# Routing's rest as a side chain, one ring of weight buffers instead of two, and the identity first, in a two-layer decoder trunk

## Chip, core and metric

One core of one Trainium2 chip runs the whole program. The metric is device time in microseconds (us). A profiled execution also gives a trace, whose span runs from its first to its last instruction. TensorE is called PE here, VectorE DVE, ScalarE ACT, GpSimd POOL; SP is the engine that issues the weight loads.

## The reference

256 tokens of width 1024 go through two layers. Layer 0 is multi-head latent attention and a dense SwiGLU, layer 1 is gated DeltaNet and a mixture of 8 experts, of which each token takes 2. The change lies in the experts and, with one edit, at the very start.

```python
def moe_ffn(h, w_router, w_gate_up, w_down):
    t = h.reshape(B * S, D)                        # 256 x 1024
    top_val, top_idx = lax.top_k(t @ w_router, 2)  # of 8
    top_w = jax.nn.softmax(top_val, axis=-1)
    combine = jnp.sum(one_hot(top_idx, 8) * top_w[..., None], axis=1)
    for e in range(8):
        gt, up = jnp.split(t @ w_gate_up[e], 2, axis=-1)      # 1024 x 2816, float32
        out = out + combine[:, e:e+1] * ((silu(gt) * up) @ w_down[e])   # 1408 x 1024
```

The eight experts' weights are 138.4 MB of float32, 17.3 MB for each expert.

## The kernel before

**Experts by size.** A sort by token count gives the eight experts seats 0 to 7. Even seats are big ("B", up to 128 tokens), odd ones small ("S", up to 64 tokens); expert 0 always has seat 0. A second pass for experts with more tokens stands in a branch that these inputs don't take. The kernel gathers each expert's tokens by a matmul with a one-hot matrix `P` (`place`, L1821, writes its columns on DVE; `gather`, L1850, does the matmuls in 9 steps), computes gate, up and down, and adds the result back by a matmul with the transpose of `P`. `places_back` (L1830) makes that transpose `SM` and the weight of every gathered token, `wsl`, which needs the routing weights `cmb2`.

**Weights.** An expert's weights come in 35 tiles of 128 x 1024 or 128 x 768 float32: 24 of gate and up, 11 of down. A big expert splits each tile in a high part (ACT cast, L197) and a low part (DVE subtraction, L198) and multiplies three times (L2046 gate and up; L1962 to L1964 down). A small expert feeds the raw tiles to PE (L2076, L1979).

**Two rings.** `wload` (L180) takes a raw buffer and issues the load on SP. Gate and up tiles take one of the 10 buffers of `wrw`; down tiles, in `down_raw` (L1931), one of the 6 of `wr2`. A load waits until the last reader of its buffer is done, and SP works in order.

**Routing.** After the router's matmul the kernel ranks the experts of each token, and positions come by a matmul (L1718 to L1724). `place(0)` and `gather(0)` make the tokens of seat 0. Then `between()`, that is `routed()` (L1755), does the rest in one piece: the second maximum and its exponential, the count per expert (`cnt`), the sort (`perm`), the arrays by seat (`chosS`, `posS`, `eidS`, `cntS`), the experts' numbers for SP (`eidi`), the routing weights (`cmb2`) and the overflow test (`mosti`). After it all the other experts' places are written, 14 instructions on DVE.

**Order.** Inside `manual_schedule` (L116 to `order.close()`, L2098) PE, DVE, ACT and POOL keep the written order among the instructions of the block. After that, and for SP throughout, the framework's planner orders the instructions by written order and by its own forecast of when each is ready; the order is then fixed.

**Side work.** While an expert's gate and up run, `sides(more)` (L2030) is called nine times (ten in a small expert), after chosen tiles, and advances every side chain by one step: the scatter of the expert before, the gather of the next group of seats (groups (0), (1,2), (3,4), (5,6,7); a group starts one expert before its first seat) and, for seat 0, `places_back()` of all eight seats.

**PSUM.** In the experts' stage 5 banks go by the tag "mm" and 3 by "acc"; the two results of a big expert's down (`y0`, `y1`) and the banks `psw` and `st` of `places_back` take "acc".

**Start.** POOL issues nine small loads (L102 to L113) and then writes the identity (L118, L119) that PE's first transpose (L141) reads.

Of the kernel before, what the change touches and what calls it, by code (L numbers as in the profile page):

```python
# [16 lines left out]
D = 1024  # L17
# [12 lines left out]
NE = 8  # L30
# [19 lines left out]
def hybrid_kernel(ctx: ExitStack, tc: tile.TileContext, rope_rows, x, c, positions, ada_w, ada_b,  # L50
# [40 lines left out]
    nc.sync.dma_start(xtok, x.rearrange("o (t p) d -> p (o t) d", p=128))  # L91

    rows = sm.tile([39, 128], F32, name="rows", bufs=1)
    r0 = 0
    col_of = {}
    for name, ap in (("nm", norm_mix.rearrange("l (k p) -> (l k) p", p=128)),
# [19 lines left out]
    order.enter_context(tc.manual_schedule(engines=MANUAL))  # L116
    ident = cst.tile([128, 128], F32)
    nc.gpsimd.memset(ident, 0.0)  # L118
    nc.gpsimd.affine_select(out=ident, in_=ident, pattern=[[-1, 128]], base=0, channel_multiplier=1,  # L119
                            compare_op=OP.not_equal, fill=1.0)  # L120
    upper = cst.tile([128, 128], F32)
# [1624 lines left out]
    tge, perm = (sm.tile([128, NE, NE], F32, name=n, bufs=1) for n in ("tge", "perm"))  # L1746
    chosS, posS = rt("chosS"), rt("posS")
    eidi = cst.tile([1, NE], I32, name="eidi")
# [6 lines left out]
    def routed():  # L1755
# [15 lines left out]
        nc.vector.tensor_copy(cnt, pt[:, 0:NE])  # L1771
        nc.vector.tensor_copy(cntm, cnt)
        nc.vector.memset(cntm[:, 0:1], -1.0)
        sq3 = [128, NE, NE]
        mine, other = cntm[:, :, None].to_broadcast(sq3), cntm[:, None, :].to_broadcast(sq3)
# [5 lines left out]
        nc.vector.tensor_tensor(perm, want[:, :, None].to_broadcast(sq3), trank[:, None, :].to_broadcast(sq3),  # L1781
                                op=OP.is_equal)
        by_turn(chosS, chos)
        by_turn(posS, pos)
        for o, v in ((eidS, eids), (cntS, cnt)):
            nc.vector.tensor_tensor(tge, perm, v[:, None, :].to_broadcast(sq3), op=OP.mult)
            nc.vector.reduce_sum(o, tge, axis=AX.X)
        nc.vector.tensor_copy(eidi, eidS[0:1, :])
        w1 = sm.tile([128, 2, 1], F32, name="w1", bufs=1)
        nc.vector.tensor_scalar(w1, w2, 1.0, None, op0=OP.add)  # L1790
        nc.vector.reciprocal(w1, w1)
        nc.vector.tensor_tensor(w2, w2, w1, op=OP.mult)
        comb = sm.tile([128, 2, NE], F32, name="comb", bufs=1)
        nc.vector.tensor_tensor(comb, chos, oh0, op=OP.subtract)
        nc.vector.tensor_tensor(comb, comb, w2.to_broadcast([128, 2, NE]), op=OP.mult)
# [4 lines left out]
        nc.vector.tensor_tensor(cmb2[:, :, :, 1], oh0, cmb2[:, :, :, 0].bitcast(F32), op=OP.subtract)  # L1800

        nc.vector.tensor_tensor(cntS, cntS, caps, op=OP.subtract)
        most = sm.tile([128, 1], F32, name="most", bufs=1)
        nc.vector.reduce_max(most, cntS, axis=AX.X)
        nc.vector.tensor_scalar(most, most, 128.0, None, op0=OP.add)
        nc.vector.tensor_copy(mosti, most[0:1, :])

    def experts(again, between):
# [20 lines left out]

        def places_back():  # L1830
            psw = acc_bank("psw")
            for e in range(NE):
                pt = acc_bank("st")
                parts = [places[e]] if kinds[e] == "B" else [places[e], places[e] + 128]
                for h, o in enumerate(parts):
                    for t in range(2):
                        pl = P[:, t, o:o + 128]
                        mm(pt[:, h * S + t * 128:h * S + (t + 1) * 128], lhsT=pl, rhs=identr, start=True, stop=True)
                        mm(psw[:, 2 * e:2 * e + 2], lhsT=pl, rhs=cmb2[:, t, e, :], start=h == t == 0,
                           stop=h == len(parts) - 1 and t == 1)  # L1840
# [4 lines left out]
            nc.vector.tensor_copy(pw, psw[:, :2 * NE].rearrange("p (e c) -> p e c", c=2))  # L1845
            nc.vector.tensor_tensor(wsl, pw[:, :, 0], pw[:, :, 1], op=OP.add)

# [83 lines left out]
        def down_raw(e, f):  # L1931
            w = moe_w_down[0, 0] if e == 0 else moe_w_down[0, bass.ds(expert_of(e), 1)].rearrange("e r c -> (e r) c")
            if kinds[e] == "S" and f == 9:

                return wload(lambda t: [(t[0:64], w[9 * 128 + 64:10 * 128, :]), (t[64:128], w[9 * 128:9 * 128 + 64, :])],
                             [128, D], ring=wr2)
            return wload(lambda t: [(t, w[f * 128:(f + 1) * 128, :])], [128, D], ring=wr2)

# [7 lines left out]

        def y_halves(e):
            if e == NE - 1:
                nc.scalar.activation(warmed, wsl[:, 0:1], AF.Sqrt, bias=eps_t, scale=0.0)
            return [sm.tile([128, D], F32R, name=n, tag=n, bufs=1) for n in ("yh", "yl")]  # L1950

        def down(e, f0, n, ah, al):
# [12 lines left out]
            if f0 + n // 128 < nf:  # L1965
                return
            yh, yl = y_halves(e)
            for q in range(2):
# [3 lines left out]
        def down_small(e, blocks):  # L1972
# [8 lines left out]
            if blocks[-1][0] == nf - 1:  # L1981
                yh, yl = y_halves(e)
                weigh(e, slice(0, 512), (yh, yl, yps[e]))
                outs.append(scatter(e, yh, yl))
# [73 lines left out]
        def expert_small(e, more):  # L2058
# [3 lines left out]
            for c0 in (0, 1024):  # L2062
# [23 lines left out]
                after()  # L2086

        if again:
            for e in range(NE):
                place(e, ps_of, chosS)  # L2090
            list(gather(0))
# [100 lines left out]
```

## Time and profile before

| what | value |
|---|---|
| runs | 1030.16, 1029.38, 1021.74 us; median 1029.38 |
| profiled execution | 1026.9 us; its span 1025.1 us |
| busy share of the span | PE 92%, DVE 66%, ACT 48%, POOL 12% |
| moved | 261.33 MB, mean 255 GB/s |
| mean granted clock of PE | 0.959 of full |

The span is 1.8 us shorter than the execution. Time 0 is the span's first instruction. The experts run from about 595 us to about 1007 us, a final norm follows. A timeline row gives start, duration, engine, line, operation, output<-input and count, and in brackets the engine's idle time before it with what released it. Matmuls of one engine overlap, so their durations don't add up.

### The profile page before, as it was taken

How to read it: one execution, taken by the hardware profiler on the slowest of the kernel's cores; microseconds unless marked ns; L12 is line 12 of the kernel's file. 1: busy time of each engine (PE TensorE's matmuls, PEld its weight loads, DVE VectorE, ACT ScalarE, POOL GpSimd, SP SyncE). 2: the span in 40 equal slices, each digit the busy share in tenths (PEclk: the TensorE clock that was granted, in tenths of full speed). 3: DMA queues.
4: the chain of work that ended last, by engine and by line, in shares of the span. 5: the costliest groups of instructions: out<-in, count | busy, mean ns of one | idle time of the engine just before them, and what ended most of it. 6: DMA issues, size and time to landing. Idle time of an engine off the chain costs nothing. (4 is left out here: it accounts for less than half of the span.)

```text
span 1025.1 us, 18883 instructions
## 1 busy us (share of the span) xinstructions
PE 941.9 (92%) x6802; PEld 752.2 (73%) x6802; DVE 673.1 (66%) x1274; ACT 490.7 (48%) x879; POOL 123.9 (12%) x226
## 2 busy tenths in 40 slices
PE   5899999999999997999999779899999899989984
PEld 3787889999999997888899768745664576457431
DVE  5788948878786778877753566625864495358232
ACT  2367546443444466555544555723742473256212
POOL 2000001000000132535633400000000000000000
PEclk9999998999999989999999877999999999999997
DMA  9959994979988846422224463789999998999992
GB/s 303 366 169 327 289 314 141 319 247 332 331 279 284 266 138 191 124 83 84 84 84 144 145 209 106 239 302 325 366 372 364 347 363 329 355 352 361 366 328 69
DMA packets 152740, 261.33 MB, mean 255 GB/s; under 512 B 13650, under 2 KB 104832, under 8 KB 152640
## 3 DMA queue, kind: packets, MB, share of 16 engines
q1 hardware_dynamic: 152336, 259.81, 74.2%
q8 instruction: 55, 0.90, 0.4%
q0 software_dynamic: 304, 0.25, 0.2%
q14 instruction: 45, 0.37, 0.1%
HBM read 258.97 MB, written 1.05 MB: 254 GB/s over the span
## 5 line engine op out<-in xcount | busy, mean ns | idle before, releaser
L461 ACT CAST whi<-w 128x1024 fp32r<-128x1024 f32 (+3 forms) x147 | 138.5, 958 | 112.7 <-PE gu L1143 45.0
L198 DVE TENSOR_TENSOR wlo<-w,whi 128x1024 fp32r<-128x1024 f32 (+1 forms) x136 | 154.5, 1158 | 43.1 <-ACT whi L197 41.4
L466 DVE TENSOR_TENSOR wlo<-w,whi 128x1024 fp32r<-128x1024 f32 (+3 forms) x132 | 148.2, 1137 | 21.1 <-ACT whi L461 20.9
L197 ACT CAST whi<-w 128x1024 fp32r<-128x1024 f32 (+1 forms) x136 | 132.2, 998 | 42.3 <-DMA w<-in_moe_w_gate_up_dram 22.8
L1142 PE MATMUL gu<-hhi,whi 128*128 128x256 f32 x336 | 95.4, 284 | 0.0
L1144 PE MATMUL gu<-hhi,wlo 128*128 128x256 f32 x336 | 95.1, 283 | 0.0
L1143 PE MATMUL gu<-hlo,whi 128*128 128x256 f32 x336 | 95.1, 283 | 0.0
L2076 PE MATMUL gu<-w,XF 128*64 128x512 f32 (+1 forms) x384 | 84.4, 564 | 0.0
L230 PE MATMUL pj<-hhi,whi 128*128 128x256 f32 x240 | 73.5, 306 | 0.0
L232 PE MATMUL pj<-hhi,wlo 128*128 128x256 f32 x240 | 68.5, 286 | 3.8 <-DVE wlo L466 3.8
L2046 PE MATMUL gu<-whi,XH 128*128 128x512 f32 x192 | 61.2, 400 | 9.4 <-ACT whi L197 9.4
L231 PE MATMUL pj<-hlo,whi 128*128 128x256 f32 x240 | 68.4, 285 | 0.0
L466 POOL TENSOR_TENSOR wlo<-w,whi 128x1024 fp32r<-128x1024 f32 x15 | 39.4, 2626 | 225.9 <-DVE al L1117 181.0
L1143 PEld LDWEIGHTS gu<-hlo,whi 128*128 128x128 f32 x336 | 64.5, 192 | 0.0
L1142 PEld LDWEIGHTS gu<-hhi,whi 128*128 128x128 f32 x336 | 64.5, 192 | 0.0
L1144 PEld LDWEIGHTS gu<-hhi,wlo 128*128 128x128 f32 x336 | 64.5, 192 | 0.0
L2046 PE MATMUL gu<-wlo,XH 128*128 128x512 f32 x192 | 60.8, 398 | 1.0 <-DVE wlo L198 0.9
L2076 PEld LDWEIGHTS gu<-w,XF 128*64 128x64 f32 x384 | 26.4, 136 | 44.7 <-issue 40.2
L2046 PE MATMUL gu<-whi,XL 128*128 128x512 f32 x192 | 58.8, 387 | 0.0
L260 DVE SCALAR_TENSOR_TENSOR adacc<-adaw,csil,adacc 128x1024 f32<-128x1024 f32 x42 | 56.2, 1337 | 2.7 <-DMA adaw<-in_ada_w_dram 2.6
L1979 PE MATMUL y<-w,at 128*64 128x512 f32 x176 | 47.2, 635 | 6.7 <-DMA w<-in_moe_w_down_dram 6.6
L1922 POOL TENSOR_TENSOR xT<-xT,part 128x256 f32<-128x256 f32 x1 | 0.7, 725 | 414.5 <-PE fx L2125 414.5
(527 smaller groups left out, 2281.6 us busy)
## 6 DMA issues: line engine op xcount, KB each, us to landing
w<-in_moe_w_down_dram SPq DMA_DIRECT2D x84, 512.0 KB, 7.4
w<-in_moe_w_gate_up_dram SPq DMA_DIRECT2D x128, 256.0 KB, 5.4
w<-in_moe_w_gate_up_dram SPq DMA_DIRECT2D x64, 512.0 KB, 7.3
adaw<-in_ada_w_dram SPq DMA_DIRECT2D x50, 512.0 KB, 5.1
w<-in_moe_w_gate_up_dram SPq DMA_DIRECT2D x128, 192.0 KB, 4.1
w<-in_ada_w_dram SPq DMA_DIRECT2D x46, 512.0 KB, 6.8
w<-in_ffn_w_gate_up_dram SPq DMA_DIRECT2D x88, 256.0 KB, 5.3
w<-in_gdn_w_in_dram SPq DMA_DIRECT2D x32, 512.0 KB, 4.6
```

Of the source, the lines that this page charges most:

```text
L197: nc.scalar.copy(dv(hi), rv(raw))
L198: eng.tensor_tensor(dv(lo), rv(raw), dv(hi).bitcast(F32), op=OP.subtract)
L230: mm(ps, lhsT=lhi, rhs=rhi, start=first, stop=False)
L231: mm(ps, lhsT=lhi, rhs=rlo, start=False, stop=False)
L232: mm(ps, lhsT=llo, rhs=rhi, start=False, stop=last)
L461: nc.scalar.copy(dv(hi), rv(raw))
L466: eng.tensor_tensor(dv(lo), rv(raw), dv(hi).bitcast(F32), op=OP.subtract)
L1142: mm(o, lhsT=h[:, c], rhs=rh, start=k == g == 0 and new, stop=False, skip_group_check=True)
L1143: mm(o, lhsT=h[:, c], rhs=rl, start=False, stop=False, skip_group_check=True)
L1144: mm(o, lhsT=l[:, c], rhs=rh, start=False, stop=k == 1 and g == 3, skip_group_check=True)
L2046: mm(p[:, :2 * m].rearrange("p (g c) -> p g c", g=2), lhsT=x[:, kk, :], rhs=w[:, k, :, o:o + m], start=kk == i == 0, stop=kk == 7 and i == 2)
L2076: mm(o, lhsT=X[:, k, :], rhs=r, start=k == 0, stop=k == 7, tile_position=(0, 64 * h))
```

## The change

```diff
     nc.sync.dma_start(xtok, ...)
+    ident = cst.tile([128, 128], F32)
+    nc.gpsimd.memset(ident, 0.0)
+    nc.gpsimd.affine_select(out=ident, ...)
     rows = sm.tile([39, 128], F32, name="rows", bufs=1)
...
     order.enter_context(tc.manual_schedule(engines=MANUAL))
-    ident = cst.tile([128, 128], F32)
-    nc.gpsimd.memset(ident, 0.0)
-    nc.gpsimd.affine_select(out=ident, ...)
...
-    def wload(srcs, shape, name="w", ring=None):
-        raw = (ring or wrw).tile(shape, F32, name=name, tag="w")
+    def wload(srcs, shape, name="w"):
+        raw = (ring[0]() if ring else wrw).tile(shape, F32, name=name, tag="w")
...
+    nload = [0]
+    def in_turn():
+        nload[0] += 1
+        return wr2 if nload[0] % 8 in (0, 3, 6) else wrw
+    ring.append(in_turn)
...
     def routed():
...
         nc.vector.tensor_copy(cnt, pt[:, 0:NE])
+        nc.vector.tensor_copy(w2s, w2)
+
+    def turns_of():
...
+        yield
         by_turn(chosS, chos)
         by_turn(posS, pos)
-        for o, v in ((eidS, eids), (cntS, cnt)):
-            ...
+        ...              # eidS alone
         nc.vector.tensor_copy(eidi, eidS[0:1, :])
+        yield
+
+    def weights_of():    # w1 to comb, as before, on w2s
...
+        yield
         by_turn(oh0, comb)
...
         nc.vector.tensor_copy(mosti, most[0:1, :])
+        yield
...
-        def places_back():
+        def places_back(es):
             psw = acc_bank("psw")
-            for e in range(NE):
+            for i, e in enumerate(es):
...
-            pw = sm.tile([128, NE, 2], F32, name="pw", bufs=1)
+            pw = sm.tile([128, NE, 2], F32, name="pw", bufs=2)
...
+            yield
...
-            return wload(lambda t: [(t, w[f * 128:(f + 1) * 128, :])], [128, D], ring=wr2)
+            return wload(lambda t: [(t, w[f * 128:(f + 1) * 128, :])], [128, D])
...
-        def y_halves(e):
+        def y_halves(e, a):
             if e == NE - 1:
-                nc.scalar.activation(warmed, wsl[:, 0:1], AF.Sqrt, bias=eps_t, scale=0.0)
+                nc.scalar.activation(warmed, a, AF.Sqrt, bias=eps_t, scale=0.0)
...
         def sides(more):
             for side in outs[:1] + more:
                 next(side, None)
+                if side in more:
+                    next(side, None)
...
+        def group(g):
+            for e in gathers[g]:
+                place(e, ps_of, ch_of)
+            yield
+            yield from gather(g)
+            yield from places_back(gathers[g])
+
+        def first_sides():
+            yield from turns_of()
+            for e in gathers[1]:
+                place(e, ps_of, ch_of)
+            yield
+            yield from weights_of()
+            yield
+            yield from gather(1)
+            yield from places_back(gathers[0])
+            yield from places_back(gathers[1])
...
             between()
-            for e in range(1, NE):
-                place(e, posS, chosS)
             order.close()
         for e in range(NE):
-            starts = [g for g, es in enumerate(gathers) if g and e == (es[0] - 1)]
-            more = [gather(g) for g in starts] + ([places_back()] if e == 0 else [])
+            more = [group(g) for g, es in enumerate(gathers) if g and e == es[0] - 1]
+            if e == 0 and not again:
+                more = [first_sides()]
             run[kinds[e]](e, more)
```

In words: `routed()` ends with the count. The sort, the weights and the overflow test become steps of a side chain of seat 0, in front of `gather(1)` and of `places_back` for seats 0, 1 and 2. The later groups' places and `places_back` run in the side chain of seat 2 or 4, before and behind their gather. Side chains other than the scatter now take two steps per call. All loads of the stage take buffers of both rings by a fixed turn, 5 of 8 from `wrw` and 3 of 8 from `wr2`, whatever they hold. The activation that fetches the table for the square root reads the last expert's own data instead of `wsl`.

## Rows read from the trace of the kernel before

**Rows 1.** The page, its slices: GB/s moved in each fortieth (25.6 us).

```profile
GB/s 303 366 169 327 289 314 141 319 247 332 331 279 284 266 138 191 124 83 84 84 84 144 145 209 106 239 302 325 366 372 364 347 363 329 355 352 361 366 328 69
```

**Rows 2.** Windows: length, busy PE, PEld, DVE, ACT, POOL; clock, DMA share, GB/s.

```profile
595.00:670.00 75.00, 63.20 (x289) 52.03 (x290) 52.15 (x107) 46.27 (x76) 0.46 (x1) 0.85 0.51 162
616.00:626.00 10.00, 9.02 (x36) 8.45 (x37) 7.06 (x26) 3.21 (x10) 0.00 (x0) 0.50 0.00 0
665.00:670.00 5.00, 3.99 (x17) 2.37 (x18) 4.03 (x6) 5.00 (x10) 0.00 (x0) 1.00 0.00 0
705.00:1000.00 295.00, 274.25 (x1269) 167.06 (x1269) 170.65 (x245) 131.76 (x199) 0.00 (x0) 0.99 0.98 354
720.00:760.00 40.00, 38.29 (x199) 30.89 (x196) 35.89 (x54) 29.13 (x47) 0.00 (x0) 1.00 1.01 372
720.00:780.00 60.00, 56.90 (x284) 38.48 (x281) 40.82 (x61) 33.69 (x54) 0.00 (x0) 1.00 1.01 374
855.00:865.00 10.00, 10.00 (x47) 5.68 (x47) 4.19 (x9) 2.68 (x6) 0.00 (x0) 1.00 0.62 226
```

**Rows 3.** PE's timeline: the first expert's stop, first matmuls of seats 0 to 3.

```profile
594.71 1.20 PE L2046 MATMUL gu<-whi,XH 128*128 128x512 f32 x2
...
608.26 0.63 PE L2046 MATMUL gu<-whi,XL 128*128 128x512 f32 x2
616.61 0.59 PE L1839 MATMUL psw<-cmb,P 128*128 128x2 f32 x2 [7.72 <-DVE cmb L1800]
...
623.48 0.78 PE L2046 MATMUL gu<-whi,XH 128*128 128x512 f32 x1
...
669.57 1.94 PE L2076 MATMUL gu<-w,XF 128*64 128x512 f32 x8
...
705.65 0.74 PE L2046 MATMUL gu<-whi,XH 128*128 128x512 f32 x2 [1.09 <-ACT whi L197]
...
760.69 1.08 PE L2076 MATMUL gu<-w,XF 128*64 128x512 f32 x4
```

**Rows 4.** Waits of SP's queue, 595 to 700 us: total, times, longest (us).

```profile
SPq L183 <- DVE wlo L198: 35.5, 11, 12.4
SPq L183 <- PE gu L2076: 13.3, 9, 10.9
```

**Rows 5.** Waits of SP's queue, 705 to 1000 us: total, times, longest (us).

```profile
SPq L183 <- PE gu L2076: 26.6, 21, 8.6
...
SPq L183 <- PE y L1979: 14.0, 7, 5.3
SPq L183 <- DVE wlo L198: 5.2, 11, 1.3
```

**Rows 6.** DVE's timeline: the loop's first split, the fourteen places.

```profile
598.73 1.23 DVE L198 TENSOR_TENSOR wlo<-w,whi 128x1024 fp32r<-128x1024 f32 x1 [2.90 <-ACT whi L197]
...
617.12 4.19 DVE L1825 TENSOR_SCALAR P<-slot,posS,chosS 128x256 fp32r<-128x256 f32 x14
```

**Rows 7.** Waits of all engines, 595 to 670 us: total, times, longest (us).

```profile
PE y L1962 <- ACT SM L1842: 1.8, 1, 1.8
```

**Rows 8.** ACT's timeline: table loads of the square root, and its next instruction.

```profile
661.52 1.28 ACT L1949 ACT_TABLE_LOAD   x1
...
1013.11 1.28 ACT L2134 ACT_TABLE_LOAD   x1
1014.40 0.29 ACT L2134 ACTIVATE stf<-stf 128x1 f32<-128x1 f32 x1
```

**Rows 9.** Timelines of POOL and PE at the start.

```profile
6.71 0.53 POOL L113 DMA_DIRECT2D vrow<-in_gdn_conv_w_dram  x1 [0.97 <-DMA rows<-in_norm_mix_dram]
7.22 0.22 POOL L118 MEMSET ident<- 128x128 f32 x1
...
7.87 0.27 PE L141 MATMUL pt<-ident,crow 8*128 8x8 f32 x1 [7.87 <-POOL ident L119]
...
14.37 0.42 PE L579 MATMUL pt<-ident,vrow 96*128 96x96 f32 x1 [2.02 <-DMA vrow<-in_gdn_conv_w_dram]
```

More of the change, by code (lines that the diff above doesn't have):

```diff
@@ L91, in hybrid_kernel @@
     nc.sync.dma_start(xtok, x.rearrange("o (t p) d -> p (o t) d", p=128))
+    ident = cst.tile([128, 128], F32)
+    nc.gpsimd.memset(ident, 0.0)
+    nc.gpsimd.affine_select(out=ident, in_=ident, pattern=[[-1, 128]], base=0, channel_multiplier=1,
+                            compare_op=OP.not_equal, fill=1.0)
     rows = sm.tile([39, 128], F32, name="rows", bufs=1)
@@ L116, in hybrid_kernel @@
     order.enter_context(tc.manual_schedule(engines=MANUAL))
-    ident = cst.tile([128, 128], F32)
-    nc.gpsimd.memset(ident, 0.0)
-    nc.gpsimd.affine_select(out=ident, in_=ident, pattern=[[-1, 128]], base=0, channel_multiplier=1,
-                            compare_op=OP.not_equal, fill=1.0)
     upper = cst.tile([128, 128], F32)
@@ L177, in col @@
         return cols[:, col_of[name] + i:col_of[name] + i + 1]
-    def wload(srcs, shape, name="w", ring=None):
-        raw = (ring or wrw).tile(shape, F32, name=name, tag="w")
+    ring = []
+    def wload(srcs, shape, name="w"):
+        raw = (ring[0]() if ring else wrw).tile(shape, F32, name=name, tag="w")
         for dst, src in srcs(raw):
@@ L1746, in hybrid_kernel @@
     tge, perm = (sm.tile([128, NE, NE], F32, name=n, bufs=1) for n in ("tge", "perm"))
-    chosS, posS = rt("chosS"), rt("posS")
+    chosS, posS, w2s = rt("chosS"), rt("posS"), rt("w2s", (128, 2, 1))
     eidi = cst.tile([1, NE], I32, name="eidi")
@@ L1771, in routed @@
         nc.vector.tensor_copy(cnt, pt[:, 0:NE])
+        nc.vector.tensor_copy(w2s, w2)
+    def turns_of():
+        sq3 = [128, NE, NE]
         nc.vector.tensor_copy(cntm, cnt)
         nc.vector.memset(cntm[:, 0:1], -1.0)
-        sq3 = [128, NE, NE]
         mine, other = cntm[:, :, None].to_broadcast(sq3), cntm[:, None, :].to_broadcast(sq3)
@@ L1782, in routed @@
                                 op=OP.is_equal)
+        yield
         by_turn(chosS, chos)
         by_turn(posS, pos)
-        for o, v in ((eidS, eids), (cntS, cnt)):
-            nc.vector.tensor_tensor(tge, perm, v[:, None, :].to_broadcast(sq3), op=OP.mult)
-            nc.vector.reduce_sum(o, tge, axis=AX.X)
+        nc.vector.tensor_tensor(tge, perm, eids[:, None, :].to_broadcast(sq3), op=OP.mult)
+        nc.vector.reduce_sum(eidS, tge, axis=AX.X)
         nc.vector.tensor_copy(eidi, eidS[0:1, :])
+        yield
+    def weights_of():
+        sq3 = [128, NE, NE]
         w1 = sm.tile([128, 2, 1], F32, name="w1", bufs=1)
-        nc.vector.tensor_scalar(w1, w2, 1.0, None, op0=OP.add)
+        nc.vector.tensor_scalar(w1, w2s, 1.0, None, op0=OP.add)
         nc.vector.reciprocal(w1, w1)
-        nc.vector.tensor_tensor(w2, w2, w1, op=OP.mult)
+        nc.vector.tensor_tensor(w2s, w2s, w1, op=OP.mult)
         comb = sm.tile([128, 2, NE], F32, name="comb", bufs=1)
         nc.vector.tensor_tensor(comb, chos, oh0, op=OP.subtract)
-        nc.vector.tensor_tensor(comb, comb, w2.to_broadcast([128, 2, NE]), op=OP.mult)
+        nc.vector.tensor_tensor(comb, comb, w2s.to_broadcast([128, 2, NE]), op=OP.mult)
         nc.vector.tensor_tensor(oh0, oh0, w1.to_broadcast([128, 2, NE]), op=OP.mult)
         nc.vector.tensor_tensor(comb, comb, oh0, op=OP.add)
+        yield
         by_turn(oh0, comb)
@@ L1800, in routed @@
         nc.vector.tensor_tensor(cmb2[:, :, :, 1], oh0, cmb2[:, :, :, 0].bitcast(F32), op=OP.subtract)
+        nc.vector.tensor_tensor(tge, perm, cnt[:, None, :].to_broadcast(sq3), op=OP.mult)
+        nc.vector.reduce_sum(cntS, tge, axis=AX.X)
         nc.vector.tensor_tensor(cntS, cntS, caps, op=OP.subtract)
@@ L1838, in places_back @@
                         mm(pt[:, h * S + t * 128:h * S + (t + 1) * 128], lhsT=pl, rhs=identr, start=True, stop=True)
-                        mm(psw[:, 2 * e:2 * e + 2], lhsT=pl, rhs=cmb2[:, t, e, :], start=h == t == 0,
+                        mm(psw[:, 2 * i:2 * i + 2], lhsT=pl, rhs=cmb2[:, t, e, :], start=h == t == 0,
                            stop=h == len(parts) - 1 and t == 1)
@@ L1843, in places_back @@
                 yield
-            pw = sm.tile([128, NE, 2], F32, name="pw", bufs=1)
-            nc.vector.tensor_copy(pw, psw[:, :2 * NE].rearrange("p (e c) -> p e c", c=2))
-            nc.vector.tensor_tensor(wsl, pw[:, :, 0], pw[:, :, 1], op=OP.add)
+            pw = sm.tile([128, NE, 2], F32, name="pw", bufs=2)
+            nc.vector.tensor_copy(pw[:, :len(es)], psw[:, :2 * len(es)].rearrange("p (e c) -> p e c", c=2))
+            nc.vector.tensor_tensor(wsl[:, es[0]:es[-1] + 1], pw[:, :len(es), 0], pw[:, :len(es), 1], op=OP.add)
+            yield
         XS = {}
@@ L1935, in down_raw @@
                 return wload(lambda t: [(t[0:64], w[9 * 128 + 64:10 * 128, :]), (t[64:128], w[9 * 128:9 * 128 + 64, :])],
-                             [128, D], ring=wr2)
-            return wload(lambda t: [(t, w[f * 128:(f + 1) * 128, :])], [128, D], ring=wr2)
+                             [128, D])
+            return wload(lambda t: [(t, w[f * 128:(f + 1) * 128, :])], [128, D])
         dpre = []
@@ L1966, in down @@
                 return
-            yh, yl = y_halves(e)
+            yh, yl = y_halves(e, ah[:, 0:1].bitcast(F32))
             for q in range(2):
@@ L1981, in down_small @@
             if blocks[-1][0] == nf - 1:
-                yh, yl = y_halves(e)
+                yh, yl = y_halves(e, blocks[-1][1][:, 0:1])
                 weigh(e, slice(0, 512), (yh, yl, yps[e]))
@@ L2086, in expert_small @@
                 after()
+        def group(g):
[14 more added lines that the diff above has]
+            yield from places_back(gathers[1])
         if again:
-            for e in range(NE):
-                place(e, ps_of, chosS)
-            list(gather(0))
+            list(group(0))
         else:
```

## The prediction

> **What bounds the kernel now.** I read the page's slices first, since one busy share hides stages. GB/s falls to between 66 and 209 in the slices from about 330 to 615 us, and is 302 to 372 in those from 666 to 999 us [rows 1]. So the experts are a stage fed by transfers, with a slow entry. The windows give sizes: from 595 to 670 us only 162 GB/s arrive, while from 705 to 1000 us it is 354, and in the best long stretch, 720 to 780 us, 374 at a DMA share of 1.01 [rows 2]. In 616 to 626 us nothing at all arrives, and PE runs at the lower of its two clock levels (0.50, that is 1.2 GHz) [rows 2].
>
> PE's timeline says why. Seat 0's first group of gate and up starts at 594.71 and issues its last matmul at 608.26; the next instruction in PE's order, `psw`, waits 7.72 us for `cmb2`, and the second group begins at 623.48 [rows 3]. In between PE does only what the routing released: transposes of places and the first of `gather(1)`. No weight tile is used up, so no buffer comes free, and SP waits for DVE's splits 35.5 us in 595 to 700, once 12.4 us [rows 4]. Seat 0 takes 594.71 to 669.57, 74.9 us; seat 2, as big, takes 705.65 to 760.69, 55.0 us [rows 3]. The entry costs some 20 us, and what follows is limited by transfers, so that an earlier entry comes out at the end.
>
> **The change, part by part.** The sum goes against the profiled execution, 1026.9 us (span 1025.1 and 1.8 around it); the median of the runs is 2.5 us higher, 1029.4.
>
> *(a) Seat 0's stop.* `psw` and `SM` move behind `gather(1)`, so PE can pass from the first group to the second without `cmb2`. What ends last then is DVE: it was busy 52.15 us in 595 to 670 [rows 2]. Of its fourteen places (4.19 us, 0.30 each [rows 6]) ten go to later seats, 3.0 us; the sort and the weights stay, as steps of two per call. That leaves 49.2 us. In 720 to 760 us, with big-expert work, DVE was busy 35.89 of 40, 0.90 [rows 2]; its first split of the loop starts at 598.73 [rows 6]. So seat 0 ends at about 598.7 + 49.2/0.90 = 653.4, against 669.57: 16.2 us. The change also adds a wait: while seat 0's last group runs, `y0` and `y1` hold two of three "acc" banks, so `psw` and `st` must take turns in the third, and every turn is a hand-over between PE and ACT or DVE. The one such hand-over before held PE 1.8 us [rows 7]; behind the waiting matmul in PE's order stand seat 0's gate and up. Most turns should fall beside other matmuls; I take 1.5 off. Value 14.7. The ends: 7.7, if only the named wait goes, and 22, if DVE had no gaps at all (598.7 + 49.2 = 647.9). I take the value near the second, as seat 2's 55.0 us, with the same splits, would also end seat 0 at 650. The square root's table, fetched in seat 0 at 661.52 because `wsl` was ready [rows 8], leaves too; its 1.28 us on ACT is inside this margin.
>
> *(b) One turn of sixteen buffers, seat 1.* Up to now gate and up can run 10 tiles ahead. For the small seat 1 that meant a full ring before its first matmul: SP waited 10.9 us for L2076 [rows 4] and nothing arrived in 665 to 670 [rows 2]. With sixteen, seat 1's sixteen wide tiles can be loaded when seat 0 ends. Left to load are then 8 tiles of 0.39 MB, 14 of 0.52 and seat 2's first, 11.0 MB, at 374 GB/s 29.4 us; with about 3 us from landing to matmul seat 2 begins at 653.4 + 32.4 + 1.5 (the hand-overs) = 687, 18.4 us before 705.65. So (b) adds 3.7. Ends: 0, and 10.9, the whole of that wait.
>
> *(c) The same, seats 2 to 7.* SP waited for buffers 26.6 + 14.0 + 5.2 = 45.8 us [rows 5], most of it with transfers still under way. In 855 to 865 us they ran dry (226 GB/s, share 0.62 [rows 2]). Were 295 us at 354 GB/s moved at 374, they would take 279, so the end is 15.8; the lower end is 0. I take 7, somewhat under half, as a window of full share can also move less. The last four down tiles, held up by the six buffers of `wr2`, are in it.
>
> *(d) The tail.* ACT fetches the square root's table at 1013.11 for 1.28 us on the chain that ends last [rows 8]; read from the last expert's own activation, it moves in front of the last down tiles, when ACT is idle. 1.3 less; at the other end 0, if the planner puts it elsewhere. The row shows 1014.40 - 1013.11 = 1.29 us until ACT's next instruction. The Trainium skill (ScalarE: Activation LUTs, What ACT_TABLE_LOAD costs) counts a drain besides and some 2.66 us in all; by it (d) would be 2.7 and the sum 1.4 lower. The row leaves no place for such a drain, so 1.3 stands.
>
> *(e) Identity first.* It takes 7.22 to 7.87 on POOL [rows 9], 0.65 us, now in front of nine load issues. PE's first transposes can start when the tokens land, at most 1.8 us sooner. But PE then waits for `vrow` until 14.37, which POOL could issue only at 6.71, after a wait for the first row load [rows 9]; pushing that load back by 0.65 pushes `vrow` back too. The first two slices move 303 and 366 GB/s [rows 1], so weights bind there. I take 0, with -1.8 and +0.65 as ends.
>
> *(f) What seats 2 and 4 get.* Ten places (3.0 us on DVE), five copies of `SM` on ACT and their matmuls, and each gather two steps at a time. Transfers cover it: DVE is at 0.58 of 705 to 1000 [rows 2]. Cost 0; without that cover 3.
>
> Sum: -14.7 - 3.7 - 7 - 1.3 = -26.7 against 1026.9, which is 1000.2; against the median 1002.7. I say 1001, and for this case 990 to 1010 (from the parts' ends taken against each other).
>
> **Rivals.**
>
> *The stream is at its limit.* Then (b) and (c) give nothing, since the dips are the memory's own, and the time is 1026.9 - 14.7 - 1.3 = 1010.9. For it: from 705 on the mean is 354 GB/s with DMA share 0.98 [rows 2]. Against: 374 over 60 us and, beside it, SP's waits for buffers [rows 2, 5]. The Trainium skill (DMA: Bandwidth & Descriptors, Where 436 GB/s comes from) sets about 358 GB/s of memory per core as what binds. By that rule the stage has 1% to win; the stretch of 374 does not agree with it.
>
> *The stop changes place.* The order is fixed from a forecast, which here was some 8 us early about `cmb2`. If `gather(1)`'s matmuls are put before their places are really written, or the second group's splits queue behind the sort on DVE, PE stops again. Then (a) keeps 5 and (b) 2: 1026.9 - 5 - 2 - 7 - 1.3 = 1011.6. For it: seat 0 is DVE's densest stretch. Against: nothing of the chain stands in PE's order before `gather(1)`, three calls later than the sort.
>
> *Slower: one ring blocks itself.* Down tiles had their own buffers and could be fetched early whatever gate and up did. In one turn, a tile whose buffer's last reader comes late holds SP, and with it every later load of either kind. A stop like seat 1's, 10.9 us of SP and 5 us without transfers [rows 2, 4], in each of eight experts costs 40 against the 16 of (a) and (d): 1051. It decides from 2 us per expert on. Against: loads are written in the order of use, so that the buffer wanted is the oldest one.
>
> *It doesn't do what it says.* The planner draws the sort and the places up again, since their inputs are ready, and order and waits stay as they are: 1027 to 1029.
>
> **How the numbers follow.** The forecast 0.55, at 1001; the stream at its limit 0.17; the stop elsewhere 0.15; no effect 0.07; the blocking ring 0.06. A measurement of this kernel can tell about 1% from no change, that is 10 us; the forecast and the first two rivals (0.87) lie below 1019, no effect within, the ring above. That makes faster 0.87, same 0.07, slower 0.06. The range reaches from 987, where (b) and (c) come near their upper ends, over both rivals to 1019; outside are the last two cases (0.13) and some 0.05 below.
>
> **What would show it.** Right: `psw` without a wait on `cmb2`, and PE's second group of seat 0 starting at about 610; L2076 first at 650 to 657; no window of 5 us without transfers between 600 and 670; seat 2 starting at 683 to 692; SP's waits for L2076 and L1979 after 705 us down by more than half, and the mean there above 360 GB/s; no table load in the final norm. Wrong: a new idle time of PE over 5 us in seat 0, released by DVE's places or by an "acc" bank; a mean of 354 GB/s or less in the later seats; SP waiting on L198 for a down tile's buffer while PE starves.

## The result and the profile after

| | before | after |
|---|---|---|
| median of the runs made together (4 each) | 1028.33 us | 994.77 us |
| lowest to highest | 1021.74 to 1030.16 | 992.42 to 997.22 |
| profiled execution, its span | 1026.9, 1025.1 us | 997.0, 995.3 us |

The ratio is 0.9685, with a 95% interval of 0.9631 to 0.9739. The forecast was 1001, the range 987 to 1019.

In after's code the split's lines are L199 (ACT) and L200 (DVE), big and small gate and up L2069 and L2099, the small down L2000, and `psw` L1859. First the slices of the page of after, each 24.9 us, to be held against [rows 1]:

```profile
GB/s 308 366 178 315 303 288 167 312 238 338 312 285 293 304 163 179 140 107 86 86 86 101 113 212 175 318 259 370 365 394 370 363 353 342 382 358 367 364 372 71
```

The last low slice of the entry moves 175 GB/s instead of 106, and the first slice above 360 begins at 672 us (27 x 24.9), where it was 718 (28 x 25.6).

The windows of after, with the columns of [rows 2]:

```profile
595.00:655.00 60.00, 55.20 (x258) 44.12 (x257) 47.55 (x107) 37.22 (x63) 0.29 (x1) 0.93 0.68 228
610.00:615.00 5.00, 4.30 (x22) 3.46 (x21) 5.00 (x21) 2.68 (x5) 0.00 (x0) 1.00 0.19 62
...
616.00:626.00 10.00, 10.00 (x55) 8.48 (x54) 10.00 (x18) 6.93 (x14) 0.00 (x0) 1.00 0.95 326
640.00:650.00 10.00, 7.35 (x33) 6.11 (x32) 6.74 (x12) 6.23 (x12) 0.00 (x0) 0.83 0.95 344
650.00:655.00 5.00, 5.00 (x25) 3.47 (x24) 0.85 (x4) 0.54 (x2) 0.00 (x0) 1.00 0.33 111
655.00:660.00 5.00, 5.00 (x25) 1.73 (x26) 0.00 (x0) 0.64 (x2) 0.00 (x0) 1.00 0.58 185
720.00:780.00 60.00, 55.48 (x270) 33.99 (x268) 31.02 (x50) 22.36 (x37) 0.00 (x0) 0.97 1.02 381
700.00:960.00 260.00, 247.34 (x1168) 156.22 (x1167) 156.11 (x227) 122.45 (x190) 0.00 (x0) 0.99 1.01 367
```

In 616 to 626 us, where nothing arrived and PE had half its clock [rows 2], 326 GB/s arrive at full clock, and DVE is busy all of the time, as PE is. That DVE sets the pace there is read from its lack of gaps, not tested by itself. The lowest 5 us between 600 and 670 are those from 610, with 62 GB/s; in 650 to 660 the transfers fall again, but not to nothing. Over 700 to 960 us the mean is 367 GB/s. The kernel before had 357 in the same window:

```profile
700.00:960.00 260.00, 244.24 (x1133) 154.49 (x1133) 160.87 (x229) 126.60 (x191) 0.00 (x0) 0.99 0.99 357
```

PE's timeline of after, in the order of [rows 3]:

```profile
594.18 1.20 PE L2069 MATMUL gu<-whi,XH 128*128 128x512 f32 x2
...
607.62 0.63 PE L2069 MATMUL gu<-whi,XL 128*128 128x512 f32 x2
608.95 0.91 PE L2010 MATMUL at<-ident,act 128*128 128x128 f32 x4 [0.70 <-DVE act L2039]
609.61 0.71 PE L2069 MATMUL gu<-whi,XH 128*128 128x512 f32 x2
...
643.19 0.38 PE L1859 MATMUL psw<-cmb,P 128*128 128x2 f32 x2 [2.65 <-ACT SM L1862]
...
653.58 1.07 PE L2099 MATMUL gu<-w,XF 128*64 128x512 f32 x2
...
689.26 0.71 PE L2069 MATMUL gu<-whi,XH 128*128 128x512 f32 x2
...
748.23 1.08 PE L2099 MATMUL gu<-w,XF 128*64 128x512 f32 x4
```

The second group starts 2 us after the first, where it was 15. Seat 0 takes 653.58 - 594.18 = 59.4 us instead of 74.9, seat 1 35.7 instead of 36.1, and seat 2 59.0 instead of 55.0, beside places and transposes that it didn't have before (more on them under e12). `psw` does wait, 2.65 us, but for a bank that ACT was still reading (`SM`), no longer for the weights.

SP's waits in after, first 595 to 700, then, below the dots, 700 to 970 us (total, times, longest):

```profile
SPq L185 <- DVE wlo L200: 28.9, 14, 11.5
SPq L185 <- PE gu L2099: 9.4, 8, 7.1
...
SPq L185 <- DVE wlo L200: 39.9, 49, 2.4
SPq L185 <- PE gu L2099: 20.6, 23, 3.4
SPq L185 <- PE y L2000: 0.8, 3, 0.4
```

Behind 700 us the total of these three has risen (61.3 us; 41.4 before), and still more arrives. What fell is the longest single wait, from 8.6 us [rows 5] to 3.4. ACT's timeline of after at the end:

```profile
971.56 1.28 ACT L1970 ACT_TABLE_LOAD   x1
972.85 0.29 ACT L1970 ACTIVATE warmed<-at,eps_t 128x1 f32<-128x1 f32 x1
979.34 0.69 ACT L1964 ACTIVATE yh<-y,wsl 128x512 fp32r<-128x512 f32 x1 [6.19 <-PE y L2000]
...
985.54 0.19 ACT L2169 ACTIVATION_READ_ACCUMULATOR junk<-fx 128x1 f32 x1
985.76 0.29 ACT L2173 ACTIVATE stf<-stf 128x1 f32<-128x1 f32 x1
```

The table arrives while ACT is idle, and the final norm's square root follows its input at once.

**A measure for the parts.** I added up the windows of 5 us from 530 us to the end of the span, the 1.05 MB of the result that is written there included, and read when 105 MB of transfers were still to come (about the end of the entry) and how long it took from there to the last 2 MB (the steady part). The kernel before: 708.1 us and 290.7 us. After: 687.8 and 281.9. So the entry gives 20.3 us and the steady part 8.8. From the last 2 MB to the end of the span there are 26.3 us before and 25.6 after, another 0.7. Seat 0 starts at 592.6 to 594.7 us in most of these traces, with no edit that bears on it, so 2 us more or less at 105 MB left need not come from an edit. The next section takes these three apart.

### The profile page after: what moved, and what is told of

Its sections match the earlier page's. It is cut to its first block, busy times and chain, and to the rows that moved or that the text cites. A ratio compares the mean times of both kernels' runs of the same rounds, so it can differ in the third digit from the quotient of the medians.

```text
span 995.3 us, 18930 instructions
## 1 busy us (share of the span) xinstructions
PE 931.6 (94%) x6802; PEld 749.5 (75%) x6802; DVE 671.4 (67%) x1281; ACT 486.2 (49%) x877; POOL 123.7 (12%) x226
## 3 DMA queue, kind: packets, MB, share of 16 engines
HBM read 258.97 MB, written 1.05 MB: 261 GB/s over the span
## 5 line engine op out<-in xcount | busy, mean ns | idle before, releaser
L200 DVE TENSOR_TENSOR wlo<-w,whi 128x1024 fp32r<-128x1024 f32 (+1 forms) x136 | 153.0, 1155 | 33.8 <-ACT whi L199 32.1
L199 ACT CAST whi<-w 128x1024 fp32r<-128x1024 f32 (+1 forms) x136 | 131.8, 998 | 35.7 <-PE gu L2069 18.5
L1146 PE MATMUL gu<-hhi,wlo 128*128 128x256 f32 x336 | 95.1, 283 | 0.0
L1145 PE MATMUL gu<-hlo,whi 128*128 128x256 f32 x336 | 95.1, 283 | 0.0
L2099 PE MATMUL gu<-w,XF 128*64 128x512 f32 (+1 forms) x384 | 85.3, 564 | 0.0
L2069 PE MATMUL gu<-whi,XH 128*128 128x512 f32 x192 | 59.4, 390 | 3.6 <-ACT whi L199 3.4
L2069 PE MATMUL gu<-wlo,XH 128*128 128x512 f32 x192 | 59.7, 392 | 2.2 <-DVE wlo L200 2.2
L2099 PEld LDWEIGHTS gu<-w,XF 128*64 128x64 f32 x384 | 26.4, 136 | 44.5 <-issue 39.5
L2069 PE MATMUL gu<-whi,XL 128*128 128x512 f32 x192 | 58.2, 385 | 0.0
L1106 PE MATMUL acc<-ah,whi 128*128 128x256 f32 x176 | 50.0, 284 | 0.0
L1107 PE MATMUL acc<-al,whi 128*128 128x256 f32 x176 | 49.8, 283 | 0.0
```

The source lines that it names most:

```text
L199: nc.scalar.copy(dv(hi), rv(raw))
L200: eng.tensor_tensor(dv(lo), rv(raw), dv(hi).bitcast(F32), op=OP.subtract)
L1145: mm(o, lhsT=h[:, c], rhs=rl, start=False, stop=False, skip_group_check=True)
L1146: mm(o, lhsT=l[:, c], rhs=rh, start=False, stop=k == 1 and g == 3, skip_group_check=True)
L2069: mm(p[:, :2 * m].rearrange("p (g c) -> p g c", g=2), lhsT=x[:, kk, :], rhs=w[:, k, :, o:o + m], start=kk == i == 0, stop=kk == 7 and i == 2)
L2099: mm(o, lhsT=X[:, k, :], rhs=r, start=k == 0, stop=k == 7, tile_position=(0, 64 * h))
```

## The experiments

All kernels compute the whole result. Each ratio is against runs of the kernel before on the same chip (medians 1024.5 to 1027.2 us).

**e1: the chain, with the two rings by kind.**

```diff
     def in_turn():
-        return wr2 if nload[0] % 8 in (0, 3, 6) else wrw
+        return wrw
...
-            return wload(..., [128, D])
+            return wload(..., [128, D], by=wr2)
```

> The changed kernel with the two rings by kind again (10 buffers for gate and up, 6 for down); side chain, identity and table fetch as changed. Two parts nearly apart (theory): seat 0 keeps its 59 us between its first matmul and seat 1's (58 to 62), the mean rate from 700 to 970 us falls from 367 GB/s to 350 to 357, and the time is 11 us above the changed kernel: 1004 to 1011 us. Rival, the entry is all: 994 to 998 us and a mean rate above 362.

Measured: 1005.96 us, ratio 0.9788 (0.9736 to 0.9841). Seat 0 takes 59.4 us, as in after; 105 MB are left at 693.0 us (15.1 us earlier than before), and the steady part, 288.9 us, is only 1.8 us shorter. From 700 to 970 us 360 GB/s arrive, more than the theory had and less than the rival.

**e2: the one turn of sixteen, with the chain as before.**

```diff
-        raw = (ring or wrw).tile(shape, F32, name=name, tag="w")
+        raw = (ring[0]() if ring else wrw).tile(shape, F32, name=name, tag="w")
...
+        return wr2 if nload[0] % 8 in (0, 3, 6) else wrw
```

> The kernel before with nothing but the one turn over sixteen buffers. Theory: PE's wait for the routing weights stays (5 us or more before psw) and seat 0 takes 70 to 76 us; from seat 2 on the transfers run at 362 GB/s or more and the last down tiles are not held up, so the time is 1013 to 1020 us. Rival, the ring is worth something only behind a fast entry: 1024 to 1030 us. Rival, one ring blocks itself: above 1032 us.

Measured: 1006.55 us, ratio 0.9793 (0.9741 to 0.9845), better than any of the theories had it. Seat 0 takes 75.0 us (592.59 to 667.59), and PE's timeline of e2 has the whole stop:

```profile
614.57 0.59 PE L1848 MATMUL psw<-cmb,P 128*128 128x2 f32 x2 [7.71 <-DVE cmb L1809]
```

105 MB are left at 700.9 us (7.2 earlier than before, 2.1 of them since seat 0 starts earlier) and the steady part takes 279.6 (11.1 less). So the turn's main gain lies where there is no stop of the chain at all.

**after_again: the changed kernel beside other variants.**

> The changed kernel once more, beside the others: 992 to 998 us. If the side chain alone (0.979) and the ring alone (0.979) added up in full it would be at 0.958 of the kernel before; the theory, that both remove part of the same idle time of the transfers around seat 1, expects 0.966 to 0.971.

Measured: 995.61 us, ratio 0.97 (0.9648 to 0.9751). Two independent parts of 0.9788 and 0.9793 would give 0.9585; so about 1% is the same microseconds, or 0.6% if the medians of the batches are set against each other (0.9810 times 0.9816 against 0.9692).

**e7 and e14: the turn with twelve buffers instead of sixteen.** The first with the chain of after, the second with the chain of before. In both, against after and e2:

```diff
-    wr2 = ...tile_pool(name="wr2", bufs=6, ...)
+    wr2 = ...tile_pool(name="wr2", bufs=2, ...)
...
-        return wr2 if nload[0] % 8 in (0, 3, 6) else wrw
+        return wr2 if nload[0] % 6 in (0,) else wrw
```

> The changed kernel with twelve buffers in one turn instead of sixteen. If the number of tiles ahead is what the ring is worth, SP's stop for L2099 at the end of seat 0 grows from 7.1 to about 12 us, transfers dry up before every small seat, and the time is 1006 to 1016 us, no better than two rings of 10 and 6. Rival, the one order is what counts and twelve do: 995 to 1000 us.

> The kernel before, with its chain as it was, but every load of the stage takes its buffer by one fixed turn, and the turn has only twelve buffers (10 and 2) where the two rings had sixteen. Theory (it is the one order that counts, since two rings by kind let one full kind hold SP and with it the other kind's loads): nearly the gain of the turn of sixteen alone (1006.55), 1006 to 1011 us, about 0.98 to 0.985 of before; the wait of psw stays at 7 to 8 us; SP waits for no raw down tile's reader (L1979's counterpart) for more than 2 us in all after 700 us. Rival (tiles ahead are what the ring gives, as the prediction's working has it): twelve over both kinds are hardly more than the ten that gate and up alone had, and four buffers are lost, so 1022 to 1035 us, no gain or a loss.

Measured: e7 997.46 us, ratio 0.9719 (0.9686 to 0.9752); e14 1010.85 us, 0.9869 (0.9845 to 0.9892). e14's time is at the upper end of what the one order was to give, its ratio just beyond it, so the rival holds a part too; `psw` waits 7.72 us there, as expected. The measure above separates what the time mixes. The last column runs from seat 7's first matmul to its last result, ACT's last `yh`:

| kernel | buffers | seat 0 starts | 105 MB left at | from there to 2 MB | seat 7 |
|---|---|---|---|---|---|
| before | 10 and 6 by kind | 594.7 us | 708.1 us | 290.7 us | 50.9 us |
| e14 | 12 in turn | 594.0 | 705.7 | 278.9 | 44.7 |
| e2 | 16 in turn | 592.6 | 700.9 | 279.6 | 46.8 |
| e1 (chain) | 10 and 6 by kind | 593.0 | 693.0 | 288.9 | 51.1 |
| e7 (chain) | 12 in turn | 592.7 | 691.0 | 281.9 | 44.9 |
| after (chain) | 16 in turn | 594.2 | 687.8 | 281.9 | 42.5 |

In the steady part twelve in one turn do all that sixteen do, 7 to 12 us against two rings by kind: there it is the one order that counts, not the number. Two rings by kind of other sizes weren't built, so that gate and up gain by having more than ten is excluded only by twelve doing as well as sixteen. In the entry the number counts, and by 3.2 to 4.8 us between twelve and sixteen. SP's timelines show what the order does. The kernel before, at the end of seat 0:

```profile
659.27 0.34 SPq L183 DMA_DIRECT2D w<-in_moe_w_down_dram  x1
670.69 15.24 SPq L183 DMA_DIRECT2D w<-in_moe_w_gate_up_dram  x22
686.18 3.59 SPq L183 DMA_DIRECT2D w<-in_moe_w_down_dram  x6
```

and after at the same place:

```profile
643.21 5.61 SPq L185 DMA_DIRECT2D w<-in_moe_w_gate_up_dram  x4
656.05 2.04 SPq L185 DMA_DIRECT2D w<-in_moe_w_down_dram  x3
658.63 9.73 SPq L185 DMA_DIRECT2D w<-in_moe_w_gate_up_dram  x16
```

With rings by kind, a load of gate and up that finds its ring full holds SP 11.1 us (659.6 to 670.69). The next down loads stand behind 22 more of gate and up; the six at 686.18 go in a row, into buffers whose readers are seat 0's splits on ACT and DVE. The last of these on DVE was done 14 us earlier:

```profile
670.89 1.22 DVE L198 TENSOR_TENSOR wlo<-w,whi 128x1024 fp32r<-128x1024 f32 x1
```

In one turn the stop is 7.2 us (648.82 to 656.05), and it is a down load that ends it. The windows of e1 and then of e7, both with the chain of after:

```profile
645.00:650.00 5.00, 5.00 (x23) 4.15 (x23) 3.47 (x6) 3.19 (x5) 0.00 (x0) 0.84 0.03 14
650.00:655.00 5.00, 5.00 (x24) 2.92 (x24) 3.21 (x6) 2.27 (x5) 0.00 (x0) 1.00 0.11 11
```

```profile
645.00:650.00 5.00, 5.00 (x23) 4.11 (x23) 1.95 (x5) 1.16 (x2) 0.00 (x0) 0.87 0.83 284
650.00:655.00 5.00, 5.00 (x25) 2.81 (x25) 0.85 (x4) 0.91 (x3) 0.00 (x0) 1.00 0.04 16
```

Two windows almost without transfers in e1, one in e7. Later in the stage the same shows in SP's longest waits for a small expert's tiles, from 700 to 970 us, first e1, then e7, where the wait for L2000 is 0.7 us in all:

```profile
SPq L185 <- PE gu L2099: 23.1, 17, 8.4
SPq L185 <- PE y L2000: 9.2, 4, 4.1
```

```profile
SPq L185 <- PE gu L2099: 17.4, 32, 3.4
```

**e3: before, with `places_back` three calls later.**

```diff
         def places_back():
+            for _ in range(3):
+                yield
```

> The kernel before with places_back put off by three calls of the side chain, so that PE's order has no psw between seat 0's first and second group; routing in one piece, all places at once, two rings. Theory A (the wait for the routing weights is the stop): PE starts the second group within 3 us of the first, seat 0 takes 59 to 63 us and the time is 1011 to 1017 us. Theory B (the one piece on DVE is the stop): PE waits instead for the places of gather(1) or for splits queued behind the routing, seat 0 takes 68 to 73 us, time 1021 to 1027 us.

Measured: 1021.63 us, ratio 0.9967 (0.9937 to 0.9996). It didn't take the wait away: the planner still put `psw` right behind the first group. PE's timeline of e3:

```profile
614.75 0.59 PE L1841 MATMUL psw<-cmb,P 128*128 128x2 f32 x2 [7.54 <-DVE cmb L1800]
```

Still, seat 0 fell to 66.0 us, 9 less than before, and only 4 of them came out at the end: seat 1 took 40.7 us instead of 36.1, and the steady part was no shorter (291.8; 290.7 before). What was wanted, the wait alone gone, wasn't reached.

**e9: all the routing in one piece, `places_back` late.**

```diff
     def routed():
...
+        list(turns_of())
+        list(weights_of())
...
         def first_sides():
-            yield from turns_of()
...
-            yield from weights_of()
```

> The changed kernel with the sort, the weights and the overflow test in one piece inside routed() again, ahead of the loop; places and transposes stay steps of the side chains, the ring stays one. Theory A (what counts is that psw and the transposes are no longer planned between seat 0's first two groups; DVE has the same work either way): seat 0 takes 58 to 63 us and the time is that of the changed kernel, 992 to 999 us. Theory B (the steps are what counts, one piece on DVE holds up the splits): a stop of 5 us or more in seat 0, which takes 65 to 72 us, time 1000 to 1008 us.

Measured: 996.09 us, ratio 0.9711 (0.9659 to 0.9763), the same as after. And that with a new stop of PE, since the planner drew all the places in front of `gather(1)`. PE's timeline of e9:

```profile
611.85 0.85 PE L1893 MATMUL xr<-P,rxh 128*128 128x192 f32 x2 [5.72 <-DVE P L1847]
```

Seat 0 takes 62.0 us, 2.6 more than after, but 105 MB are left at 688.2, as in after. So cutting the routing into steps is not what brings the chain's gain. What e9 shares with after is that `places_back` comes behind `gather(1)` and is spread over seats 0, 2 and 4.

**e4: everything that after leaves to seats 2 and 4 goes back into seat 0.**

```diff
         def group(g):
-            for e in gathers[g]:
-                place(e, ps_of, ch_of)
-            yield
             yield from gather(g)
-            yield from places_back(gathers[g])
...
-            for e in gathers[1]:
+            for e in range(1, NE):
                 place(e, ps_of, ch_of)
...
-            yield from places_back(gathers[0])
-            yield from places_back(gathers[1])
+            for es in gathers:
+                yield from places_back(es)
```

> The changed kernel with the places and the transposes of all eight seats in seat 0's side chain (as steps, after gather(1)), and only the gathers left to seats 2 and 4. Theory (DVE sets seat 0's pace): 3.0 us more on DVE and five more turns of psw and st in one bank make seat 0 3 to 8 us longer, 997 to 1003 us in all. Rival, this work was hidden in seat 0 too: 993 to 996 us.

Measured: 1000.50 us, ratio 0.9748 (0.9698 to 0.9798). Seat 0 is only 1.9 us longer than in after, less than the theory's 3 to 8. Seat 1 takes 46.6 us instead of 35.7, and between its matmuls `psw` and `st` of the late seats take turns in one bank. PE's waits for that bank are 2.1 us in all; how the rest of the 10.9 us arises isn't shown. PE's timeline of e4, in seat 1:

```profile
664.13 1.08 PE L2099 MATMUL gu<-w,XF 128*64 128x512 f32 x4
666.52 2.29 PE L1859 MATMUL psw<-cmb,P 128*128 128x2 f32 x10 [1.31 <-ACT SM L1862]
668.75 1.97 PE L2099 MATMUL gu<-w,XF 128*64 128x512 f32 x4
```

Four matmuls of the small expert take 1.08 us before the wait and 1.97 after it, and the window there shows the clock at the lower of its two levels (0.50):

```profile
667.00:671.00 4.00, 4.00 (x15) 2.37 (x15) 1.71 (x4) 0.42 (x1) 0.00 (x0) 0.50 0.75 235
```

In return the steady part is the shortest of all, 277.1 us.

**e10: the later groups one expert earlier, in the small seats 1 and 3.**

```diff
-            more = [group(g) for g, es in enumerate(gathers) if g and e == es[0] - 1]
+            more = [group(g) for g, es in enumerate(gathers) if g and e == es[0] - (1 if again else 2)]
```

> The changed kernel with the side chains of groups 2 and 3 (places, gather, transposes) started one seat earlier, in the small seats 1 and 3 instead of the big seats 2 and 4. Theory (with one ring the big seats are now paced by DVE, for which SP waited 39.9 us from 700 to 970 us): SP's waits for L200 fall below 20 us, seat 2's and seat 4's windows on DVE get lighter by 7 us each, and the time is 989 to 993 us. Rival, the transfers alone pace the stage: 994 to 997 us. Rival, the turns of psw and st in one bank hold up the small seats' matmuls as they did with all eight seats' transposes: 998 to 1004 us.

Measured: 998.77 us, ratio 0.9728 (0.9677 to 0.9779), some 3 us over after in the same batch (997.66 to 998.98 against 994.42 to 996.43). Seat 1 takes 43.1 us instead of 35.7. SP's waits for L200 from 700 to 970 us fell to 30.7, not below 20. The time is in the range of the last rival, but gathers moved with the transposes, so the bank isn't shown to be the cause.

**e12: only places and transposes moved to the small seats 1, 3 and 5.**

```diff
         def group(g):
-            for e in gathers[g]:
-                place(e, ps_of, ch_of)
-            yield
             yield from gather(g)
-            yield from places_back(gathers[g])
...
+                more += {1: [other_places()], 3: [late_back(2)], 5: [late_back(3)]}.get(e, [])
```

> The changed kernel with the places of seats 3 to 7 written in the small seat 1 and the transposes of groups 2 and 3 made in the small seats 3 and 5; the gathers stay in the big seats 2 and 4. Theory (the moved places and transposes were not free in the big seats: from 35 MB arrived to 137.5 MB the changed kernel took 281 us, the kernels with this work in seat 0 took 276 to 278): 276 to 279 us for that stretch, 990 to 994 us in all. Rival, free as predicted: 994 to 997 us.

Measured: 994.34 us, ratio 0.9682 (0.9642 to 0.9723). Seat 2 falls from 59.0 to 54.1 us, and nothing of it shows in the time. The moved work alone doesn't make seat 2 long, though: e1 and e7 have it there and take 54.9 and 54.5. Counted from seat 0's first matmul they start seat 2 2.4 us later than after does, and seat 3 1.5 to 2 us sooner.

**e13: e12 with a seventeenth buffer.**

```diff
-    wr2 = ...tile_pool(name="wr2", bufs=6, ...)
+    wr2 = ...tile_pool(name="wr2", bufs=7, ...)
...
-        return wr2 if nload[0] % 8 in (0, 3, 6) else wrw
+        return wr2 if nload[0] % 17 in (0, 2, 5, 7, 10, 12, 15) else wrw
```

> The same with a seventeenth buffer. Theory (SP's stop of 7.1 us at the end of seat 0 is a full ring): the stop falls by about the 1.4 us of one tile, and the time by 0 to 2 us against sixteen buffers, which is at the edge of what can be told: 988 to 994 us.

Measured: 992.81 us, ratio 0.9673 (0.9639 to 0.9707). It is the lowest median, but its runs (991.83 to 994.53) overlap with those of e12 and after. The stop didn't fall: SP's longest wait for L2099 there is 7.2 us, against 6.4 in e12.

**e5: the identity back in its old place.**

```diff
-    ident = cst.tile([128, 128], F32)      # ahead of the row loads
...
     order.enter_context(tc.manual_schedule(engines=MANUAL))
+    ident = cst.tile([128, 128], F32)
```

> The changed kernel with the identity written behind POOL's nine load issues again. Theory (the start is set by the last of these loads and by the weights): same time within 1 us, 994 to 997 us, and PE's transpose of vrow within 0.6 us of 13.8 us. Rival, the earlier transposes are worth their 1.8 us or more: 997 to 999 us.

Measured: 994.36 us, ratio 0.9689 (0.9647 to 0.9731), the same as after within the spread of the runs (992.29 to 998.06). PE's timeline at the start, after and then e5:

```profile
2.60 0.27 PE L141 MATMUL pt<-ident,crow 8*128 8x8 f32 x1 [2.60 <-POOL ident L95]
...
13.79 0.42 PE L581 MATMUL pt<-ident,vrow 96*128 96x96 f32 x1 [3.39 <-DMA vrow<-in_gdn_conv_w_dram]
```

```profile
8.10 0.27 PE L141 MATMUL pt<-ident,crow 8*128 8x8 f32 x1 [8.10 <-POOL ident L119]
...
13.83 0.30 PE L581 MATMUL pt<-ident,vrow 96*128 96x96 f32 x1 [1.73 <-DMA vrow<-in_gdn_conv_w_dram]
```

PE's first matmul comes 5.5 us earlier, and the one that needs `vrow` at the same time.

## Why the prediction was right, step by step

One reading of its start was off and bears on nothing behind it: the low slices move 83 to 209 GB/s and begin at 359 us, not 66 to 209 from 330 [rows 1].

**(a) Seat 0's stop.** Predicted: seat 0 ends at 653.4 plus 1.5 for hand-overs, 14.7 less. Measured: it ends at 653.58 and is 15.5 shorter, and the single wait for a bank is 2.65 us. In the stream of transfers the chain gives 15.1 us (e1 against before) or 13.1 (after against e2); counted from seat 0's first matmul, 13.4 and 14.7. DVE was the engine to count in a part of the seat: in 616 to 626 us it has no gap, in 640 to 650 it is busy 6.74 of 10. The working took a share of 0.90 for it throughout; it was 47.55 of 60 us, 0.79, with less work than the 49.2 counted, so the agreement to a microsecond is partly luck. e9 and e4 keep most of the gain with the routing in one piece and with all the places in seat 0; and the turn doesn't shorten seat 0 (75.0 us in e2, 74.9 in e14). What e9 and e4 share with after is `psw` and the transposes behind `gather(1)`, and two steps per call, which no run tests alone.

**(b) The turn at the entry.** Predicted 3.7. Measured at 105 MB left: 5.2 with the chain, 7.2 without; counted from seat 0's first matmul, 6.4 and 5.1. That sixteen tiles ahead do more than ten was the right reason here, since e7 and e14, with twelve, lose 3.2 and 4.8 of it. Seat 2 starts at 689.26, where 687 was forecast and 683 to 692 named as right: 16.4 us earlier than before, not 18.4. Against e1 the turn brings seat 2's start forward by 2.5 us, from 97.6 to 95.1 behind seat 0's. One detail was wrong: SP still stops for 7.2 us in seat 1, as sixteen buffers also fill up.

**(c) The turn in the later seats.** Predicted 7, from waits of which somewhat under half were to come back. Measured in the steady part: 7.0 with the chain (e1 to after), 11.1 without. With twelve buffers the gain there is the same, so it isn't their number; what e7 and e14 share with after is that no kind has a ring of its own to hold SP with.

(c) also counted the last down tiles in, and there PE gets most of it: seat 7 takes 50.9 us before, 51.1 in e1 and 42.5 in after. Timelines of SP and PE, with the last four down loads, PE's last matmuls of down tiles and, for the kernel before, the window at its end; before and then after:

```profile
991.67 3.11 SPq L183 DMA_DIRECT2D w<-in_moe_w_down_dram  x4
...
1000.87 5.73 PE L1979 MATMUL y<-w,at 128*64 128x512 f32 x12 [3.44 <-DMA w<-in_moe_w_down_dram]
...
1000.00:1005.00 5.00, 4.05 (x10) 1.12 (x12) 0.00 (x0) 0.00 (x0) 0.00 (x0) 0.50 0.40 105
```

```profile
961.52 2.47 SPq L185 DMA_DIRECT2D w<-in_moe_w_down_dram  x4
...
970.48 8.80 PE L2000 MATMUL y<-w,at 128*64 128x512 f32 x40
```

Before, PE waits 3.44 us for these tiles and runs its last twelve matmuls in 5.73 us, with a granted clock of 0.50 in 1000 to 1005, the lower of the two levels. After, the loads are out before PE needs them, and 40 matmuls run through in 8.80 us. From seat 2's first matmul to seat 7's first it is 250.1 us before and 247.6 after. So PE gains 2.5 us up to seat 7 and 8.5 in it, 11.0 where 7 was predicted; 9.5 of them are the turn's (after against e1). The mechanism was right and the size too small.

Here a sign that I had named failed. SP's waits for the small experts' tiles were to fall by more than half behind 700 us. From 700 to 970 us they fell from 36.2 (26.6 and 9.6) to 21.4, and together with those for DVE's splits they rose from 41.4 to 61.3, while more arrived. So the total of SP's waits doesn't tell their cost; whether the transfers in flight run out under a wait does.

**(d) The tail.** Predicted 1.3. From the last `yh` to the square root there were 7.70 us:

```profile
1006.70 0.69 ACT L1943 ACTIVATE yh<-y,wsl 128x512 fp32r<-128x512 f32 x1 [16.14 <-PE y L1979]
```

(to 1014.40 [rows 8]), and there are 6.42 (979.34 to 985.76): 1.28 less. The Trainium skill (ScalarE: Activation LUTs, What ACT_TABLE_LOAD costs) counts a drain besides, some 2.66 us in all; this case shows none of it.

**(e) Identity.** Predicted 0, and e5 shows no difference clear of the noise, for the reason given: `vrow` comes through POOL's queue when it did before. The end of -1.8 had the first transposes too late, as PE's first matmul comes 5.5 us earlier, but the wait for `vrow` takes all of it up.

**(f) The rest in seats 2 and 4.** Predicted 0, 3 without cover. Seat 2 is about 4 us longer than before. The steady part of after is 281.9 us (283.1 and 282.2 in after_again and e5), against 279.6 in e2 and 277.1 in e4, which do that work in seat 0; that would be 2 to 6 us. But e12, which takes it out of seat 2, gains nothing that can be measured (281.9, 994.34 us). So whether it costs these few microseconds stays open.

**Sum.** -26.7 was predicted against the profiled execution; it fell by 29.9. By PE's timetable, which differs from that of the transfers (20.3 at 105 MB left, 8.8 behind it), seat 2 starts 16.4 us earlier (predicted 14.7 + 3.7), seats 2 to 7 take 11.0 less (7), and from the last `yh` to the end it is 2.4 less, 1.3 of it the table. The remaining 1.2 us, behind the square root, I can't put down to an edit. So the sum came near because (a) and (b) were 2.0 too large together and (c) 4.0 too small, which is partly luck.

**The parts alone.** They don't add as the working had it. It gives the turn without the chain 3.7 + 7 = 10.7 us; e2 gained 18.9 by the medians (18.3 by the trace at the last 2 MB, 2.1 of it an earlier start of seat 0). The chain alone should give 16.0 and gave 19.5. Together they give 0.6 to 1% less than the product. Part of it shows: the turn is worth 11.1 us of the steady part without the chain and 7.0 with it.

**The rivals.** *The stream at its limit* gave 1010.9 and is refuted: the stream moves 367 GB/s instead of 357 over 260 us, and 381 in 720 to 780. The Trainium skill (DMA: Bandwidth & Descriptors, Where 436 GB/s comes from) has about 358 per core as what binds; here one core took more for 260 us. *The stop changes place* happened only in e9, 5.72 us long, with no loss that can be told at the end. *One ring blocks itself*: no stop of that size came, and the two rings had the longer ones. *No effect*: PE's order did change, though e3 shows that the planner can draw such work up again.

## What to carry to other kernels

Where one queue issues in order, separate buffer rings by kind can block each other, since a load that waits for a full ring holds every other one behind it. Here one turn in the order of use was better even with fewer buffers (e7 against e1, e14 against before). Their number counted where nothing was released for a long stretch, at the entry. Judge a wait of the queue by whether the transfers dry up in that window, not by its length or the total of waits, and look at the last tiles, which nothing behind them covers. Side work that hands a PSUM bank back and forth came with a longer seat 1 in e4 and e10, and with no loss of time in seats 3 and 5 (e12). In a stage that is fed by transfers, an engine's stop of 5 us may cost nothing, as in e9.

## What was not expected of the hardware

Over 260 us one core moved 367 GB/s in after and 372 in e4. In e4 two waits of PE, 0.83 us up to 663.54 and 1.31 up to 666.52, are followed by a granted clock of 0.50 in 667 to 671, with ten short matmuls at its start. No run parts the waits from the short matmuls; I had counted neither as a danger for the clock.
